# A float32 decoder layer on one core: first block product's operands from ScalarE and VectorE, block products in fixed order, plain down sums copied by VectorE

## The chip, the cores and the metric

The kernel runs on 1 core of one Trainium2 chip. The metric is the device time of one execution in microseconds (us). A core has a matrix engine (TensorE, PE in the profile), a vector engine (VectorE, DVE), an activation engine (ScalarE, ACT), a general engine (GpSimd, POOL) and a queue that issues most DMAs (SyncE, SP). Each engine runs its own list of instructions in a fixed order and waits at the head of that list; DMAs run beside them. TensorE's sums lie in banks of PSUM, everything else in SBUF.

## The reference

One decoder layer on x (1024 tokens by 1024 channels), all in float32:

```python
x = x + 0.5 * post1(swiglu_1(pre1(x)))
x = x + post_mix(hybrid_mixer(pre_mix(x)))
x = x + 0.5 * post2(swiglu_2(pre2(x)))

def swiglu(x, w_gate, w_up, w_down):          # 1024 -> 2816 -> 1024
    return (jax.nn.silu(x @ w_gate) * (x @ w_up)) @ w_down
```

`pre` and `post` are RMS norms with a gain. The mixer (a stick-breaking attention group beside an RWKV-7 group) is not touched by the change. The two feed-forward parts, FFN1 and FFN2, are the same code with other weights.

## The kernel before

A float32 product is made of three matmuls (`mm3`, L123): each operand is split into a rounded part "hi" and a rest "lo" = value - hi, and hi·hi, hi·lo, lo·hi add up in one PSUM bank. So each weight block and each activation block is first made into a pair of tiles, `wh` and `wl` for weights.

**Up part of an FFN** (`Ffn.up`, L463). The 2816 hidden channels are 22 blocks f of 128. Blocks f = 0 and 1 are "plain": two halves h of the tokens, each a gate product (bank X) and an up product (bank Z). `plain_evac` (L350) takes them out: Silu of the gate sum on ScalarE, times the up sum on VectorE, then `split` (hi on ScalarE, lo on VectorE) and two DMAs to DRAM (`hf_d`), through one tile `e{f}_{h}`. Blocks f = 2 to 21 go as 2x2 block matrices with seven products instead of eight. `product(f)` (L428) issues them as n = 1, 2, 5, 6, 4, 7, 3, 12 matmuls each; n = 1, 6 and 7 share the bank X, which ScalarE copies out between them (`f1p` L423 after n = 1, `f1u` L439 after n = 6, `f1v` L444 after n = 7). They need two sets of combined operands:
- for the inputs, once per FFN, `combine` (L240): nine sums of 128x2048 on VectorE and the four splits (hi on ScalarE, lo on VectorE) of n = 5, 6, 4 and 7, in a pool `xr` of five buffers R0 to R4;
- for the weights, for every f, `prep(f)` (L300): `load(f)` brings the raw gate and up block (`f1r`, 512 KB each), VectorE makes four sums of 128x512, hi goes to ScalarE for n = 2, 6, 7 and to GpSimd for the others, and all seven lo to GpSimd. `prep(f + 1)` runs beside `product(f)`; only f = 2 has no product to run beside.

After the sums, the space of `xr` goes to a pool `fu` (L463 on), which holds the tiles of the product stage, every fifth pair `wh`, `wl` among them.

**Down part** (`ffn_down`, L491). The hidden blocks f = 0 and 1 are a plain product (`f1df`): 16 groups of six matmuls through two banks A, each copied to the accumulator tile `f1acc` (L555). The others are seven products again, in steps (c, i): n = 1, 2, 5, 6, 3, 7, 4 (`f1dX`, `f1dZ`, `f1dY`), whose sums VectorE adds to `f1acc` (L511). Their weights are prepared by `prep(c, ...)` (L519): four loads `f1B`, sums on GpSimd (`f1T`, `f1B`), seven `f1dwh` on ScalarE (L536) and seven `f1dwl` on GpSimd (L537). The hidden operands `f1ho` are loaded by `hload` (L540).

The order in which instructions of the program's different parts stand on an engine is made by a scheduler, by when it reckons their inputs to be there; `tc.keep_in_program_order` pins an instruction to the order of the program. Names with f2 are the same tiles in FFN2. `x2x`, `x2X6p` and `x2X4h` belong to the norm and transposition of FFN2's input, which run while its plain products have begun.

## Time and profile before

| | us |
|---|---|
| median of 3 runs | 2215.29 |
| lowest, highest | 2211.8, 2218.39 |
| the profiled execution | 2211.98 |
| its span (first to last instruction) | 2210.3 |
| PE busy | 2094.5 (95%) |
| DVE, POOL, ACT busy | 1329.6, 1108.3, 817.2 |

All times in the rows are us from the start of the span of that one execution. A row of a timeline gives the start, the duration, the engine, the line, the operation with its output and input, and in brackets the idle time just before it with what ended it. Durations of neighbours overlap by a little, so what an instruction costs in a row of its kind is the distance of the starts. The granted TensorE clock (PEclk) is given as a share of full speed; it takes two levels, 1.2 and 2.4 GHz, so 0.50 is a stretch wholly at the lower one.

### The profile page before, as it was taken

Reading aid. Unit: us, or ns where it says so; the run is one execution under the profiler, and the core shown is the slowest. Engines: PE = TensorE matmul, PEld = TensorE weight load, DVE = VectorE, ACT = ScalarE, POOL = GpSimd, SP = SyncE. Lnnn points to the kernel's source line nnn. Section 1 sums busy time; section 2 is a strip of 40 time slices with the busy share of each in tenths; the row PEclk is TensorE's granted clock in tenths of the full one; section 3 lists DMA queues with packets and bytes.
Section 4 is the critical chain, followed back from the end, with each engine's and each line's share of the span. In section 5 each row is a group of like instructions: output and inputs, shape, how many; then the busy total and the mean of one; then the engine's idle time right before and its main releaser. Section 6 shows DMA issues by size and latency. Waiting matters only on the chain.

```text
span 2210.3 us, 30206 instructions
## 1 busy us (share of the span) xinstructions
PE 2094.5 (95%) x10976; PEld 1719.9 (78%) x10976; DVE 1329.6 (60%) x1873; ACT 817.2 (37%) x1412; POOL 1108.3 (50%) x897
## 2 busy tenths in 40 slices
PE   8899999989999999999999999898799999998998
PEld 6678888868887777687888887777678888877886
DVE  7667777624546545735537778546676767733556
ACT  5233333332105533324136667436323333332102
POOL 2866666658542345245211111221686666647734
PEclk9999999999999999999989999999899999999999
DMA  5244555568764355164665572443235555566765
GB/s 153 76 124 130 164 141 157 153 213 307 225 215 146 78 168 172 48 181 140 192 150 159 174 217 87 157 129 115 76 100 149 161 153 146 160 225 204 254 212 190
DMA packets 415476, 353.82 MB, mean 160 GB/s; under 512 B 35169, under 2 KB 337249, under 8 KB 415329
## 3 DMA queue, kind: packets, MB, share of 16 engines
q1 hardware_dynamic: 406800, 347.45, 52.3%
q10 hardware_dynamic: 8528, 4.46, 0.9%
q8 instruction: 87, 1.43, 0.3%
q14 instruction: 61, 0.49, 0.1%
HBM read 224.96 MB, written 126.88 MB: 159 GB/s over the span
## 4 chain that ended last, share of the span: by engine, by line
PE 76%; DVE 9%; issue 4%; ACT 4%; POOL 4%; DMA 2%; SPq 0%; DVEq 0%; ACTq 0%; POOLq 0%
PE pj L124 3%; PE pj L126 2%; PE pj L125 2%; PE f2X L124 2%; PE f1X L124 2%; PE f2X L125 2%; PE f2X L126 2%; PE f1X L126 2%; PE f1X L125 2%; PE a_512o L1430 2%; PE f2DY L125 2%; PE f1DY L125 2%; PE f2DY L124 2%; PE f1DY L126 2%; PE f2DY L126 2%
## 5 line engine op out<-in xcount | busy, mean ns | idle before, releaser
L112 POOL TENSOR_SCALAR wh<-wr 128x1024 fp32r<-128x1024 f32 x54 | 62.3, 1155 | 280.1 <-PE wod L126 66.1
L319 POOL TENSOR_TENSOR f1wl<-f1r,f1wh 128x512 fp32r<-128x512 f32 x100 | 141.2, 1424 | 15.9 <-ACT f1wh L316 12.7
L319 POOL TENSOR_TENSOR f2wl<-f2r,f2wh 128x512 fp32r<-128x512 f32 x100 | 139.3, 1406 | 13.0 <-ACT f2wh L316 9.7
L113 POOL TENSOR_TENSOR wl<-wr,wh 128x1024 fp32r<-128x1024 f32 x54 | 136.6, 2532 | 3.1 <-PE pj L126 0.2
L318 POOL TENSOR_SCALAR f2wh<-f2r 128x512 fp32r<-128x512 f32 x60 | 68.5, 1147 | 107.4 <-PE f2pX L125 38.8
L318 POOL TENSOR_SCALAR f1wh<-f1r 128x512 fp32r<-128x512 f32 x60 | 60.0, 1005 | 91.6 <-PE f1X L125 27.0
L511 DVE TENSOR_TENSOR f1acc<-f1dX,f1acc 128x512 f32<-128x512 f32 x64 | 44.3, 692 | 76.8 <-PE f1dX L126 76.8
L511 DVE TENSOR_TENSOR f2acc<-f2dX,f2acc 128x512 f32<-128x512 f32 x64 | 44.3, 692 | 76.5 <-PE f2dX L126 76.5
L1409 POOL TENSOR_SCALAR a_0B<-a_512B 128x1 f32<-128x1 f32 x32 | 15.4, 482 | 131.4 <-DVE a_512B L1410 98.8
L124 PE MATMUL pj<-x1X4h,wh 128*128 128x512 f32 x176 | 75.5, 429 | 0.5 <-DVE tw L925 0.5
L124 PE MATMUL pj<-x1X2h,wh 128*128 128x512 f32 x176 | 72.3, 411 | 0.6 <-DVE qkl L1120 0.5
L126 PE MATMUL pj<-x1X4h,wl 128*128 128x512 f32 x176 | 70.5, 401 | 0.0
L125 PE MATMUL pj<-x1X4l,wh 128*128 128x512 f32 x176 | 69.6, 396 | 0.0
L125 PE MATMUL pj<-x1X2l,wh 128*128 128x512 f32 x176 | 69.4, 395 | 0.0
L126 PE MATMUL pj<-x1X2h,wl 128*128 128x512 f32 x176 | 69.4, 394 | 0.0
L319 POOL TENSOR_TENSOR f1wl<-f1S,f1wh 128x512 fp32r<-128x512 f32 x40 | 63.1, 1587 | 1.6
L319 POOL TENSOR_TENSOR f2wl<-f2S,f2wh 128x512 fp32r<-128x512 f32 x40 | 62.4, 1569 | 1.7
L537 POOL TENSOR_TENSOR f2dwl<-f2B,f2dwh 128x1024 fp32r<-128x1024 f32 x20 | 47.6, 2406 | 20.0 <-ACT f2dwh L536 20.0
L537 POOL TENSOR_TENSOR f1dwl<-f1B,f1dwh 128x1024 fp32r<-128x1024 f32 x20 | 47.6, 2401 | 19.4 <-ACT f1dwh L536 19.4
L124 PE MATMUL wod<-wh,ymh 128*128 128x512 f32 x128 | 51.6, 403 | 1.1 <-DVE woacc L196 1.1
L126 PE MATMUL wod<-wh,yml 128*128 128x512 f32 x128 | 50.2, 395 | 0.6 <-DMA yml<-yl_d 0.6
L125 PE MATMUL wod<-wl,ymh 128*128 128x512 f32 x128 | 50.4, 394 | 0.0
(1448 smaller groups left out, 7098.7 us busy)
## 6 DMA issues: line engine op xcount, KB each, us to landing
f1ho<-f1hs_d SPq DMA_DIRECT2D x112, 256.0 KB, 4.6
f2ho<-f2hs_d SPq DMA_DIRECT2D x112, 256.0 KB, 4.0
f1hs_d<-f1h SPq DMA_DIRECT2D x56, 256.0 KB, 3.3
f1hs_d<-f1l SPq DMA_DIRECT2D x56, 256.0 KB, 3.0
f2hs_d<-f2h SPq DMA_DIRECT2D x56, 256.0 KB, 3.0
f2hs_d<-f2l SPq DMA_DIRECT2D x56, 256.0 KB, 2.9
wr<-in_w_in_dram SPq DMA_DIRECT2D x27, 512.0 KB, 3.9
f1r<-in_ffn_w_gate_dram SPq DMA_DIRECT2D x19, 512.0 KB, 4.9
```

Source lines behind the costliest of these rows:

```text
L112: nc.gpsimd.tensor_scalar(wh, raw, 1.0, 0.0, op0=ALU.mult, op1=ALU.add)
L113: nc.gpsimd.tensor_tensor(wl, raw, wh, op=ALU.subtract)
L124: nc.tensor.matmul(ps, lhsT=lh, rhs=rh, start=first, stop=False, **kw)
L125: nc.tensor.matmul(ps, lhsT=lh, rhs=rl, start=False, stop=False, **kw)
L126: nc.tensor.matmul(ps, lhsT=ll, rhs=rh, start=False, stop=last, **kw)
L318: nc.gpsimd.tensor_scalar(wh, src[n], 1.0, 0.0, op0=ALU.mult, op1=ALU.add)
L319: nc.gpsimd.tensor_tensor(wl, src[n], wh, op=ALU.subtract)
L511: nc.vector.tensor_tensor(quarter(tt, n), ps, quarter(tt, n), op=ALU.add)
L537: nc.gpsimd.tensor_tensor(wl, src[n], wh, op=ALU.subtract)
L1409: nc.gpsimd.tensor_scalar(B[:, w:w + 1], iv, 1.0, 0.0, op0=ALU.mult, op1=ALU.add)
L1430: nc.tensor.matmul(po[:, 0:P], lhsT=t.AT[:, k * P:(k + 1) * P], rhs=V[:, t.z0 // P + k, :], start=t.first and k == 0, stop=t.last and k == ...
```

## The change

Four things are changed, in both FFNs unless said otherwise.
- `prep_first(2)` takes the place of `prep(2)`: the weights of f = 2 get their sums and all lo parts on VectorE and all hi parts on ScalarE, none on GpSimd. It is a generator that is run in pieces between the pieces of `combine`. `load(3)` is issued before them instead of after `combine`.
- The plain tiles of the second token half (`e0_1`, `e1_1`) become one tile `ev`, a sixth one in the pool `xr` of five buffers; before, they lay in the pool `WP`. FFN2 (`late=True`) pins its first Silu.
- The first matmul of each k = 0 group of a block product is pinned, in `Ffn.mm` and in the down part's `mm`.
- The 16 copies of the plain down sums go from ScalarE (L555) to VectorE (L583).

```diff
-    def mm3(ps, lh, ll, rh, rl, first, last, **kw):
-        nc.tensor.matmul(ps, lhsT=lh, rhs=rh, start=first, stop=False, **kw)
+    def mm3(ps, lh, ll, rh, rl, first, last, pin=False, **kw):
+        i = nc.tensor.matmul(ps, lhsT=lh, rhs=rh, start=first, stop=False, **kw)
+        if pin:
+            tc.keep_in_program_order(i)
...
             lo(4, r2)
+            self.ev = rp.tile("xr", f"{self.nm}ev", [P, 2, 1024])
             yield
...
+        def prep_first(self, f):
+            G, U = self.raw.pop(f)
+            S = self.fr.tile("S", f"{self.nm}S{f}", [P, 1024])
+            S1, S2 = [self.half(S, i) for i in range(2)]
+            A11, A12, A21, A22 = G[:, 0:4], G[:, 4:8], U[:, 0:4], U[:, 4:8]
+            sums = {5: (S1, A21, A22, ALU.add), 6: (S2, S1, A11, ALU.subtract),
+                    7: (A21, A11, A21, ALU.subtract), 3: (A12, A12, S2, ALU.subtract)}
+            src = {1: A11, 2: A12, 5: S1, 6: S2, 4: A22, 7: A21, 3: A12}
+            for i, n in enumerate(PO):
+                if n in sums:
+                    d, x, y, op = sums[n]
+                    nc.vector.tensor_tensor(d, x, y, op=op)
+                wh, wl = self.slot()
+                nc.scalar.copy(wh, src[n])
+                nc.vector.tensor_tensor(wl, src[n], wh, op=ALU.subtract)
+                self.op[f, n] = wh, wl
+                if i % 2:
+                    yield
...
                 mm3(ps, wh[:, k, :], wl[:, k, :], xh[:, k, :], xl[:, k, :], first and k == 0, k == 3,
-                    skip_group_check=True)
+                    pin=k == 0, skip_group_check=True)
...
-            t = WP.tile("wr", f"{self.nm}e{f}_{h}", [P, 1024])
+            t = self.ev[:, f] if h else WP.tile("wr", f"{self.nm}e{f}_{h}", [P, 1024])
             s, hv = t[:, 0:HT], t[:, HT:]
-            nc.scalar.activation(s, pg, AF.Silu)
+            i = nc.scalar.activation(s, pg, AF.Silu)
+            if self.late and f == h == 0:
+                tc.keep_in_program_order(i)
...
-            comb = self.combine()
+            comb, first = self.combine(), self.prep_first(2)
             self.plain_mm(0, 1)
             self.plain_evac(0, 0)
             self.plain_evac(1, 0)
+            self.load(3)
+            next(first)
             next(comb)
+            next(first)
             self.plain_mm(1, 1)
             next(comb)
-            self.prep(2)
+            next(first)
+            next(first, None)
+            next(comb, None)
             self.plain_evac(0, 1)
             self.plain_evac(1, 1)
-            next(comb, None)
             self.fu = Pool(self.nm + "u", dict(wh=1, wl=1, tp=3, hv=6, sh=3, sl=2, s1=1))
-            self.load(3)
...
-                nc.scalar.copy(quarter(tt, n), ps)
+                nc.vector.tensor_copy(quarter(tt, n), ps)
...
-    F2 = Ffn("f2", a["ffn2_w_gate"][0], a["ffn2_w_up"][0], a["ffn2_w_down"][0])
+    F2 = Ffn("f2", a["ffn2_w_gate"][0], a["ffn2_w_up"][0], a["ffn2_w_down"][0], late=True)
```

**ScalarE at the start of FFN1's block products, before.** `f1e` is a plain tile, `f1r_2` and `f1r_3` the raw weights of f = 2 and 3, `f1p` the copy of bank X after n = 1; the second number of a name tells tiles apart.

```order
L360 CAST f1e_1_623<-f1e_1_623 128x512
L316 CAST f1wh_606<-f1S_596 128x512
L316 CAST f1wh_612<-f1r_2_449 128x512
L360 CAST f1e_1_630<-f1e_1_630 128x512
L423 COPY f1p_702<-f1X_676 128x512
L425 ACTIVATE f1p_702<-f1p_702 128x512
L435 COPY f1y_719<-f1DY_706 128x512
L316 CAST f1wh_653<-f1r_3_643 128x512
L439 COPY f1u_733<-f1X_676 128x512
```

**The same place after.**

```order
L339 CAST f1wh_616<-f1r_2_449 128x512
L339 CAST f1wh_624<-f1r_2_447 128x512
L385 CAST f1ev<-f1ev 128x512 x2
L319 CAST f1wh_658<-f1S_646 128x512
L319 CAST f1wh_652<-f1r_3_515 128x512
L448 COPY f1p_701<-f1X_675 128x512
L460 COPY f1y_718<-f1DY_705 128x512
L450 ACTIVATE f1p_701<-f1p_701 128x512
L319 CAST f1wh_664<-f1r_3_517 128x512
L464 COPY f1u_732<-f1X_675 128x512
```

Two splits of f = 3 (`f1wh_658`, `f1wh_652`) now stand ahead of the first copy out of bank X; `f1wh_652` lies in the pool `fu`, on the space that `ev` had, and waits until the four DMAs that write `ev` to DRAM have landed.

**SyncE's queue at the same place, before** (`f1e_1`, after it `f1ev`, is the second token half's plain result on its way to DRAM; `f1r_3`, `f1r_4` raw weights):

```order
L366 DMA f1hf_d<-f1e_0_508 128x4x128 x2
L366 DMA f1hf_d<-f1e_1_623 128x4x128 x2
L285 DMA f1r_4_672<-in_ffn_w_gate_dram 128x8x128
L366 DMA f1hf_d<-f1e_1_630 128x4x128
L285 DMA f1r_3_643<-in_ffn_w_gate_dram 128x8x128
L366 DMA f1hf_d<-f1e_1_630 128x4x128
L285 DMA f1r_4_674<-in_ffn_w_up_dram 128x8x128
L285 DMA f1r_3_645<-in_ffn_w_up_dram 128x8x128
```

**and after:**

```order
L288 DMA f1r_3_515<-in_ffn_w_gate_dram 128x8x128
L391 DMA f1hf_d<-f1e_0_508 128x4x128 x2
L288 DMA f1r_3_517<-in_ffn_w_up_dram 128x8x128
L288 DMA f1r_4_671<-in_ffn_w_gate_dram 128x8x128
L288 DMA f1r_4_673<-in_ffn_w_up_dram 128x8x128
L391 DMA f1hf_d<-f1ev 128x4x128 x4
```

The loads of f = 3 and f = 4 now stand ahead of the writes of the second token half.

**PE in the plain down part of FFN1, before:** the first matmuls of the seven products stood among the plain ones.

```order
L126 MATMUL f1df_5_3876<-wh_3721,f1hf 128x512
L124 MATMUL f1dZ_4003<-f1dwh_3770,f1ho_3927 128x512
L125 MATMUL f1dZ_4003<-f1dwl_3771,f1ho_3927 128x512
L126 MATMUL f1dZ_4003<-f1dwh_3770,f1ho_3927 128x512
L124 MATMUL f1dZ_4003<-f1dwh_3770,f1ho_3927 128x512
L125 MATMUL f1dZ_4003<-f1dwl_3771,f1ho_3927 128x512
L126 MATMUL f1dZ_4003<-f1dwh_3770,f1ho_3927 128x512
L124 MATMUL f1dY_4011<-f1dwh_3774,f1ho_3929 128x512
L124 MATMUL f1df_5_3884<-wh_3727,f1hf 128x512
```

**and after:**

```order
L128 MATMUL f1df_5_3875<-wh_3720,f1hf 128x512
L124 MATMUL f1df_5_3883<-wh_3726,f1hf 128x512
L127 MATMUL f1df_5_3883<-wl_3727,f1hf 128x512
L128 MATMUL f1df_5_3883<-wh_3726,f1hf 128x512
L124 MATMUL f1df_5_3883<-wh_3726,f1hf 128x512
L127 MATMUL f1df_5_3883<-wl_3727,f1hf 128x512
L128 MATMUL f1df_5_3883<-wh_3726,f1hf 128x512
```

The seven matmuls of `f1dZ` and `f1dY` moved behind the last `f1df`, after the first six of `f1dX`; FFN2 moves alike.

## Rows read from the trace of the kernel before

**Rows 1.** The page: busy time by engine, and the chain by engine.

```profile
PE 2094.5 (95%) x10976; PEld 1719.9 (78%) x10976; DVE 1329.6 (60%) x1873; ACT 817.2 (37%) x1412; POOL 1108.3 (50%) x897
...
PE 76%; DVE 9%; issue 4%; ACT 4%; POOL 4%; DMA 2%; SPq 0%; DVEq 0%; ACTq 0%; POOLq 0%
```

**Rows 2.** Waits of PE, whole span: who for whom, total us, times, longest.

```profile
PE f2X L124 <- POOL f2wh L318: 10.9, 2, 8.0
PE f2df L124 <- ACT f2acc L555: 6.1, 2, 4.5
```

**Rows 3.** Timeline of PE: FFN1's first block product to its third.

```profile
70.07 0.39 PE L124 MATMUL f1X<-X_0h,f1wh 128*128 128x512 f32 x1
...
91.36 0.80 PE L124 MATMUL f1X<-X_1h,f1wh 128*128 128x512 f32 x1 [4.92 <-ACT f1u L439]
...
125.37 0.39 PE L126 MATMUL f1DY<-X_1h,f1wl 128*128 128x512 f32 x1
125.60 0.39 PE L124 MATMUL f1X<-X_0h,f1wh 128*128 128x512 f32 x1
```

**Rows 4.** Timeline of SP's queue, FFN1's up part.

```profile
35.63 39.72 SPq L366 DMA_DIRECT2D f1hf_d<-f1e  x6
```

**Rows 5.** Timeline of POOL, FFN1's first weight split.

```profile
53.78 15.36 POOL L318 TENSOR_SCALAR f1wh<-f1r 128x512 fp32r<-128x512 f32 x1 [24.72 <-PE f1pX L125]
```

**Rows 6.** Timeline of DVE at the end of FFN1's input sums.

```profile
65.77 2.28 DVE L256 TENSOR_TENSOR f1L<-f1R,f1H 128x2048 fp32r<-128x2048 f32 x1
67.97 0.68 DVE L307 TENSOR_TENSOR f1S<-f1r 128x512 f32<-128x512 f32 x1
68.57 0.68 DVE L355 TENSOR_TENSOR f1e<-f1pZ,f1e 128x512 f32<-128x512 f32 x1
```

**Rows 7.** DMA issues from 70 to 100: KB each, median us to landing.

```profile
f1hf_d<-f1e SPq DMA_DIRECT2D x4, 256.0 KB, 3.2
```

**Rows 8.** The same from 84.5 to 86.2: the last of these writes.

```profile
f1hf_d<-f1e SPq DMA_DIRECT2D x1, 256.0 KB, 6.3
```

**Rows 9.** Timeline of PE: FFN2's transposes, first and third block product.

```profile
1539.31 0.69 PE L163 MATMUL x2X6p<-ident,x2x 128*128 128x128 f32 x2 [2.88 <-ACT x2x L666]
...
1574.58 0.80 PE L124 MATMUL f2X<-x2X2h,f2wh 128*128 128x512 f32 x1 [8.02 <-POOL f2wh L318]
...
1627.98 0.39 PE L124 MATMUL f2X<-x2X2h,f2wh 128*128 128x512 f32 x1
```

**Rows 10.** Timeline of ACT, in the norm of FFN2's input.

```profile
1531.74 1.28 ACT L354 ACT_TABLE_LOAD   x1
```

**Rows 11.** Timeline of DVE: the first of FFN2's input sums.

```profile
1546.76 2.28 DVE L258 TENSOR_TENSOR f2R<-x2X2h,x2X2l 128x2048 f32<-128x2048 f32 x1
```

**Rows 12.** Timeline of PE, FFN1's plain down part.

```profile
468.81 0.39 PE L124 MATMUL f1df<-wh,f1hf 128*128 128x512 f32 x1
...
489.18 0.50 PE L125 MATMUL f1dZ<-f1dwl,f1ho 128*128 128x512 f32 x1 [3.70 <-POOL f1dwl L537]
...
495.38 0.80 PE L124 MATMUL f1df<-wh,f1hf 128*128 128x512 f32 x1 [4.53 <-ACT f1acc L555]
...
504.90 0.39 PE L124 MATMUL f1dX<-f1dwh,f1ho 128*128 128x512 f32 x1
```

**Rows 13.** Windows: us, busy (count) PE, PEld, DVE, ACT, POOL, then PEclk, DMA share, GB/s.

```profile
495.00:500.00 5.00, 4.62 (x11) 3.66 (x12) 0.00 (x0) 3.32 (x6) 5.00 (x3) 0.50 0.04 12
```

**Rows 14.** Timeline of POOL, FFN1's plain down part.

```profile
493.73 2.34 POOL L537 TENSOR_TENSOR f1dwl<-f1T,f1dwh 128x1024 fp32r<-128x1024 f32 x1
496.03 7.07 POOL L537 TENSOR_TENSOR f1dwl<-f1B,f1dwh 128x1024 fp32r<-128x1024 f32 x3
```

**Rows 15.** Timeline of SP's queue at the same place.

```profile
501.19 8.11 SPq L544 DMA_DIRECT2D f1ho<-f1hs_d  x11
```

**Rows 16.** DMA issues from 501.0 to 501.5.

```profile
f1ho<-f1hs_d SPq DMA_DIRECT2D x1, 256.0 KB, 4.6
```

**Rows 17.** Timeline of DVE, FFN1's plain down part.

```profile
506.53 0.69 DVE L511 TENSOR_TENSOR f1acc<-f1dX,f1acc 128x512 f32<-128x512 f32 x1 [34.06 <-PE f1dX L126]
```

More of the change, by code (lines that the diff above doesn't have):

```diff
@@ L220, in layer_kernel, with __init__ @@
     class Ffn:
-        def __init__(self, nm, wg, wu, wd):
-            self.nm = nm
+        def __init__(self, nm, wg, wu, wd, late=False):
+            self.nm, self.late = nm, late
             self.wg = wg.rearrange("(k p) f -> p k f", p=P)
@@ L566, in mm @@
                 mm3(ps, ho[n][:, 0, k, :], ho[n][:, 1, k, :], wh[:, k, :], wl[:, k, :], first and k == 0, k == 1,
-                    skip_group_check=True)
+                    pin=k == 0, skip_group_check=True)
         for s_, (c, i) in enumerate(steps):
```

## The prediction

> **What bounds the kernel now.** I read the page first, then the waits of PE, then the timelines at the places that the change touches. PE is busy 95% of the span and is 76% of the chain that ended last [rows 1]: the kernel is bound by TensorE, and an edit pays only where it takes away a gap of PE, or a stretch at the lower clock behind a gap. Neighbouring matmuls stand 0.227 us apart at the upper clock [rows 3], so a block product of 12 takes 2.72 us and one f of seven 19.04 us. At the lower clock the distance is about 0.43 us (4.62 us busy for 11) [rows 13]. The change moves no matmul away; it can give back only gaps, and there are four places with them.
>
> **FFN1, start of the block products.** The first one starts at 70.07, right behind the plain products, and that of f = 4, from where PE runs without gaps, at 125.60 [rows 3]. Two f's need 38.1 us, so 108.2 would be the end without loss: 17.4 us are lost. The longest single gap, 4.92 us, waits for a copy of bank X on ScalarE [rows 3], which stood behind a split of f = 3 whose raw weights came late: their loads stood on SP behind writes, one of which held the queue's head for most of 39.72 us [rows 4]. After: `load(3)` is out of that queue's jam, and f = 2's operands come out of VectorE's own list. VectorE's cost per 128x2048 sum is 2.20 us and per 128x512 0.60 us (distances of starts) [rows 6]. From 54.76, where the sum ahead of the new instructions ends (five such steps before 65.77), stand 7 large and 16 small ones up to the last lo of `ev`: 7 x 2.20 + 16 x 0.60 = 25.0, so it ends at 79.8. Products n = 1, 2, 5 find their operands in time and run from 70.07 to 78.2. Then comes the **new wait**: n = 6 adds to bank X, which `f1p` must have left; `f1p` stands on ScalarE behind the split `f1wh_652`, and that waits until all four writes of `ev` have landed. On SP these stand behind the loads of f = 4. A write lands in 3.2 us as the median, in 6.3 us when it stands among loads [rows 7, 8]. The last write is issued at about 80.2, so it lands between 83.4 and 86.5; I take 85.2, because the loads stand right ahead of it. The split and the copy (0.6 us each, as the small DVE ones) follow: n = 6 starts at 86.4, a gap of 8.2 us. Behind a gap of 4.5 us the trace shows a stretch of 5 us at the lower clock [rows 12, 13], 12 matmuls at 0.43 instead of 0.227: 2.4 us. Products n = 6, 4, 7, 3 take 10.9 us, so f = 2 ends at 99.7, and f = 3, whose raw weights and operands are there by then, at 118.7. That is 125.6 - 118.7 = **7 us won** (3 to 11: the landing -1.8 or +1.3, and up to 4 us of gaps that f = 3 may keep).
>
> What GpSimd did for f = 2 is gone, 7 lo and 4 hi. Its first split took 15.36 us [rows 5], from 53.78 to 69.1, while VectorE ran sums with two SBUF inputs without a gap, and it ended when VectorE turned to a row with a PSUM input at 68.57 [rows 6]. So f = 3's first splits on GpSimd will not start before the `ev` rows that read PSUM, about 76.8. They are needed at 99.7, so this is covered.
>
> The Trainium skill, "Perfetto Trace Analysis", section "Optimizing Scalar/DVE Operations", speaks against this part: as GpSimd and VectorE share an SBUF read port, moving work between these two might not help. By that rule the starts' gain of 14.3 us would fall away, and the time would be 2204. The trace agrees that the two collide, by the 15.36 us above; what that can cost here, by rows, is the first rival.
>
> **FFN2, the same place.** Silu no longer stands between the norm's square roots; one table load is 1.28 us [rows 10], four of them go, two on the way to the last transposes, and with them two Silu of 0.60. So `x2x` comes over 3.2 us earlier, which covers the transposes' wait of 2.88 us [rows 9]: they start at 1536.4. The plain products behind them lose a stretch at the lower clock too. They ended at 1574.58 - 8.02 = 1566.56; without the 2.88, a further 0.35 and about 3 us of lower clock at 1560.2. VectorE's sums started at 1546.76 [rows 11], now about 4.5 earlier. 12 large, 20 small and 3 of 0.4 us are 39.6 us, the last lo of `ev` at 1581.9, landed at 1587, n = 6 at about 1588.4. Products 1, 2, 5 run 1560.2 to 1568.4, so the **gap is 20 us**, where the old one was 8.02 ahead of n = 1 with smaller ones after. n = 4, which stood ahead of n = 6 before, can't fill it since the order is pinned. From 1588.4: 10.9 + 2.4 + 19.0 gives f = 4 at 1620.7 against 1627.98 [rows 9]: **7.3 us won** (3 to 11).
>
> **The two plain down parts.** Before, PE ran from 468.81 to 504.90 with gaps of 3.70 (GpSimd's `f1dwl`) and 4.53 (the copies on ScalarE, behind `f1dwh` casts) and 5 us at the lower clock [rows 12, 13]. After, the copies are on VectorE, which was idle there for 34.06 us [rows 17]: 16 x 0.69 us beside a group of six matmuls of 1.36 us each, so they are hidden; without that cover 0.69 us a group. The 96 plain matmuls then end at 468.81 + 21.8 = 490.6. **What is late next** is GpSimd's chain, which doesn't change: it hands out the fourth `f1dwl` at 496.07 and the next three 2.36 us apart [rows 14], against 1.36 us that PE takes for a product. n = 1, 2, 5 run until 494.7, n = 6 waits 1.2, n = 3 and 7 wait 0.9 each, until 501.9. Next on PE is n = 1 of the second step; its `f1ho` load is issued at 501.19, behind a weight load on SP that waits for the same chain, and lands 4.6 us later [rows 15, 16]: a gap of 3.9. It runs from 505.8 to 507.1, and n = 4 of the first step to 508.5. Before, the same work ended at 504.90 + 41 x 0.227 = 514.2. 5.7 us won; gaps of 7 us in 11 may bring the lower clock again (-2.4). I take **4.5 for each FFN** (2.5 to 7); FFN2's gap behind the copies is as long, 4.5 [rows 2], and its timeline is the same to a few tenths.
>
> A copy on VectorE has one input, in PSUM; the adds of L511, which read PSUM too, ran beside GpSimd's chain at its 2.4 us a row [rows 14, 17], so I add nothing for GpSimd. The pins move no other matmul: elsewhere PE's list is what it was.
>
> **The sum.** 7 + 7.3 + 2 x 4.5 = 23.3 us off the profiled execution's 2211.98: 2188.7. Its median sister runs are 3.3 us slower; halfway between the two bases, I forecast 2190. The ends of the four terms, which will hardly all fall on one side, give 11 to 36 us.
>
> **The rivals.**
> 1. *VectorE and GpSimd collide, so that `ev` ends later.* Once VectorE reads PSUM, GpSimd gets in, and VectorE's small rows stretch. GpSimd can run only four rows of f = 3 before it needs `ev` gone: two of 0.6 and two of 1.25 us, so `ev` is at most 3.7 us later per FFN: 3.3 + 3.6 + 9 = 16 us, 2197. For it: the 15.36 us [rows 5]. Against: VectorE waits only if GpSimd is in first.
> 2. *The wait for `ev` doesn't bind* (f = 3's split finds room elsewhere). Then f = 2 and 3 run through: 17.4 in FFN1, and in FFN2 from 1568.4 the sums still hold n = 4 to about 1574 and the plain end stands at 1560.2, f = 4 at 1604: 24. With 9: 50 us, 2163. Against: the wait stands in the list.
> 3. *Slower: f = 3 starves behind the late n = 6.* GpSimd's splits of f = 3's n = 5 wait for the same landing, and all later ones queue behind. If they miss f = 3's turn, PE gets gaps like those of before in f = 3, some 6 us, and 3 at the lower clock per FFN; with a landing 6 us later the starts lose 7.5 each, the down parts keep 5 in all: 10 us slower, 2223. It decides from where the landing is some 12 us later than I put it in both FFNs. Against: 13 us lie between the landing and f = 3.
> 4. *The change doesn't do what it says:* in FFN1 the first product was on time already, so a ready first operand gives nothing there; if also the down parts only trade ScalarE's wait for GpSimd's, within 5 us of before.
>
> **How the numbers follow.** Forecast 0.72, rival 1 0.12, rival 2 0.06, rival 3 0.05, rival 4 0.05. The range 2178 to 2205 takes in rival 1 and most of the ends. A measurement can tell some 0.3% (6.6 us) from no change. Faster 0.88 (forecast nearly whole, rivals 1 and 2), same 0.07, slower 0.05.
>
> **What would show it.** Right: a gap of about 8 us ahead of n = 6 of f = 2 in FFN1 and about 20 in FFN2, put down to ScalarE's copy `p2` or the landing; no 8 us gap ahead of FFN2's n = 1; transposes x2X6p without a wait; plain down sums without a gap and 1 to 4 us gaps on GpSimd's `dwl` and the `ho` load behind them; f = 4 at about 119, and in FFN2 at about 1609 (1620.7, less the 11.5 won ahead of it). Wrong: gaps in f = 3, VectorE rows stretched before `ev`, GpSimd's down chain slower than 2.4 us a row, or gaps at places that the change doesn't touch.

## The result, and the profile after

The changed kernel takes 2189.66 us (median; 2188.91 to 2190.37), the kernel before 2213.9 beside it. The ratio is 0.9885, 95% interval 0.9865 to 0.9905: faster by 1.15%. The forecast was 2190.0.

The page of the changed kernel: its span, the busy times and the chain by engine.

```profile
span 2187.6 us, 30180 instructions
...
PE 2082.1 (95%) x10976; PEld 1714.0 (78%) x10976; DVE 1341.7 (61%) x1919; ACT 800.5 (37%) x1384; POOL 1057.3 (48%) x875
```

Against [rows 1] PE lost 12.4 us of busy time (stretches at the lower clock are busy time too), GpSimd 51 us of work, and the span is 22.7 us shorter. The waits of PE (engine, tile and line, who it waited for: total us, times, longest) answer to [rows 2]:

```profile
PE f2X L124 <- ACT f2p L448: 18.0, 1, 18.0
PE f1X L124 <- ACT f1p L448: 7.7, 1, 7.7
...
PE f2dX L124 <- DMA f2ho<-f2hs_d: 4.0, 1, 4.0
PE f1dX L124 <- DMA f1ho<-f1hs_d: 3.8, 1, 3.8
...
PE f1dX L127 <- POOL f1dwl L565: 1.9, 2, 1.3
```

The rows of before are gone, and these new ones stand in their place: one wait ahead of n = 6 in each FFN, and small ones in the down parts.

To see where the time went I cut the span at starts of PE's instructions that both kernels have. **S1**: start of the span to n = 1 of f = 4 in FFN1. **D1**: first `f1df` to the second step's `f1dZ`. **M**: from there to the first `f2pX` of FFN2's plain products (the rest of FFN1's down part, 188.8 to 189.0 us in every kernel here, then norms and mixer, where no code was changed). **S2**: from there to n = 1 of f = 4 in FFN2. **D2**: as D1, in FFN2. The three stretches left over (the products from f = 4 on, twice, and the tail) are 343.2, 343.2 and 194.1 us in every kernel here, to 0.6 us, but for two places told below (the runs f3_later and own_queue). All times are of one profiled execution each:

| kernel | S1 | D1 | M | S2 | D2 | median |
|---|---|---|---|---|---|---|
| before | 125.60 | 45.47 | 995.53 | 118.17 | 45.10 | 2213.9 |
| after | 119.03 | 42.63 | 992.86 | 110.32 | 42.29 | 2189.7 |
| copies_only | 127.78 | 42.81 | 1002.96 | 120.29 | 42.32 | 2208.5 |
| copies_back | 118.32 | 46.38 | 994.06 | 108.48 | 46.52 | 2198.0 |
| free_order | 111.33 | 41.67 | 992.11 | 103.48 | 42.60 | 2180.8 |
| no_ev_wait | 116.55 | 42.38 | 996.30 | 109.21 | 42.91 | 2188.8 |
| lo_on_gpsimd | 127.44 | 42.87 | 997.59 | 118.32 | 42.08 | 2211.2 |
| silu_free | 118.36 | 42.10 | 993.00 | 113.73 | 41.90 | 2196.6 |
| ho_ahead | 119.14 | 36.26 | 993.54 | 111.16 | 35.44 | 2176.9 |
| down_gaps | 118.86 | 42.57 | 1000.65 | 110.98 | 43.46 | 2190.4 |
| f3_later | 114.08 | 41.77 | 992.04 | 104.50 | 43.53 | 2183.6 |
| free_ho_ev | 108.97 | 36.39 | 999.20 | 100.74 | 36.43 | 2164.2 |
| own_queue | 117.78 | 42.07 | 993.52 | 109.35 | 41.82 | 2188.1 |
| load3_only | 120.84 | 44.60 | 1001.60 | 115.90 | 44.47 | 2207.3 |

Before to after: S1 6.57, D1 2.84, S2 7.85, D2 2.81 us shorter, 20.1 in all. The other 2.67 of the span's 22.7 lie in M, in the mixer and the norms, where nothing was changed: M ranges from 992.0 to 1003.0 over these executions. Two windows of the same 50 us of the mixer, before and copies_only, show how (PE busy with count, granted clock, DMA share, GB/s). Before:

```profile
1200.00:1250.00 50.00, 47.64 (x403) 0.97 0.63 183
```

and copies_only:

```profile
1200.00:1250.00 50.00, 46.67 (x361) 0.86 0.54 154
```

The same code (its start differs by under 3 us) ran 42 matmuls fewer at a granted clock of 0.86 instead of 0.97. So a median carries some us of this, and the stretches S and D of a trace show an edit more finely than the medians do. They scatter too. Where the up part is that of the changed kernel (after, copies_back, ho_ahead, down_gaps), S1 is 118.3 to 119.1 and S2 108.5 to 111.2; where the down part is (after, no_ev_wait, lo_on_gpsimd, silu_free, own_queue), D1 is 42.1 to 42.9 and D2 41.8 to 42.9. Before and copies_only, with one up part, differ by 2.2 in S1 and 2.1 in S2. So a difference of 1 us in one stretch, and of 2 in S2, shows nothing by itself.

**FFN1's start after**, PE (answers to [rows 3]):

```profile
70.53 0.39 PE L124 MATMUL f1X<-X_0h,f1wh 128*128 128x512 f32 x1
...
86.55 0.79 PE L124 MATMUL f1X<-f1H,f1wh 128*128 128x512 f32 x1 [7.69 <-ACT f1p L448]
...
91.79 0.40 PE L124 MATMUL f1DW<-f1H,f1wh 128*128 128x512 f32 x1
...
119.03 0.39 PE L124 MATMUL f1X<-X_0h,f1wh 128*128 128x512 f32 x1
```

One gap of 7.69 us ahead of n = 6, its 12 matmuls at the lower clock (86.55 to 91.79, 5.24 us instead of 2.72), then f = 2 and 3 without a gap. What held it, on VectorE, SP and ScalarE:

```profile
78.45 1.28 DVE L310 TENSOR_TENSOR f1S<-f1r 128x512 f32<-128x512 f32 x1
79.66 2.76 DVE L386 TENSOR_TENSOR f1ev<-f1ev 128x512 fp32r<-128x512 f32 x2
82.34 0.68 DVE L311 TENSOR_TENSOR f1S<-f1S,f1r 128x512 f32<-128x512 f32 x1
```

```profile
76.80 0.37 SPq L288 DMA_DIRECT2D f1r<-in_ffn_w_gate_dram  x1
77.36 0.43 SPq L288 DMA_DIRECT2D f1r<-in_ffn_w_up_dram  x1
78.67 4.13 SPq L391 DMA_DIRECT2D f1hf_d<-f1ev  x4
```

```profile
83.11 0.62 ACT L319 CAST f1wh<-f1S 128x512 fp32r<-128x512 f32 x1 [3.87 <-DVE f1S L311]
85.39 0.62 ACT L319 CAST f1wh<-f1r 128x512 fp32r<-128x512 f32 x1 [1.66 <-DMA f1hf_d<-f1ev]
85.91 0.58 ACT L448 COPY f1p<-f1X 128x512 f32<-128x512 f32 x1
```

ScalarE stands 1.66 us for the landing of `ev`, and before that 3.87 us for VectorE's sum, which stands behind the last lo of `ev` on VectorE's list.

**FFN1's down part after**, PE (answers to [rows 12]), and the granted clock of a window behind the last gap:

```profile
489.69 0.50 PE L127 MATMUL f1dX<-f1dwl,f1ho 128*128 128x512 f32 x1 [1.26 <-POOL f1dwl L565]
...
492.02 0.50 PE L127 MATMUL f1dY<-f1dwl,f1ho 128*128 128x512 f32 x1 [0.67 <-POOL f1dwl L565]
...
494.36 0.50 PE L127 MATMUL f1dX<-f1dwl,f1ho 128*128 128x512 f32 x1 [0.67 <-POOL f1dwl L565]
...
499.62 0.79 PE L124 MATMUL f1dX<-f1dwh,f1ho 128*128 128x512 f32 x1 [3.83 <-DMA f1ho<-f1hs_d]
...
504.83 0.40 PE L124 MATMUL f1dZ<-f1dwh,f1ho 128*128 128x512 f32 x1
```

```profile
500.00:505.00 5.00, 5.00 (x13) 0.53 1.03 388
```

The 96 plain matmuls run without a gap, the four gaps are those of the forecast, and the 12 matmuls behind the last one ran at the lower clock (0.53, against 0.50 in [rows 13]).

### The profile page after: what moved, and what is told of

The parts are those of the page before. It is cut to its first block, busy times and chain, and to the rows that moved or that the text cites. A ratio compares the mean times of both kernels' runs of the same rounds, so it can differ in the third digit from the quotient of the medians.

```text
span 2187.6 us, 30180 instructions
## 1 busy us (share of the span) xinstructions
PE 2082.1 (95%) x10976; PEld 1714.0 (78%) x10976; DVE 1341.7 (61%) x1919; ACT 800.5 (37%) x1384; POOL 1057.3 (48%) x875
## 4 chain that ended last, share of the span: by engine, by line
PE 77%; DVE 12%; ACT 4%; issue 3%; POOL 2%; DMA 2%; SPq 0%; DVEq 0%; ACTq 0%; POOLq 0%
PE pj L124 3%; PE f1X L124 3%; PE f2X L124 3%; PE f1X L128 2%; PE f1X L127 2%; PE f2X L127 2%; PE f2X L128 2%; PE pj L128 2%; PE pj L127 2%; PE f2DY L124 2%; PE f1DY L128 2%; PE f1DY L124 2%; PE f2DY L127 2%; PE f1DY L127 2%; PE f2DY L128 2%
## 5 line engine op out<-in xcount | busy, mean ns | idle before, releaser
L322 POOL TENSOR_TENSOR f1wl<-f1r,f1wh 128x512 fp32r<-128x512 f32 x95 | 130.5, 1386 | 13.0 <-ACT f1wh L319 9.7
L322 POOL TENSOR_TENSOR f2wl<-f2r,f2wh 128x512 fp32r<-128x512 f32 x95 | 130.5, 1386 | 13.0 <-ACT f2wh L319 9.7
L321 POOL TENSOR_SCALAR f2wh<-f2r 128x512 fp32r<-128x512 f32 x57 | 59.4, 1047 | 115.8 <-PE f2pZ L127 47.7
L321 POOL TENSOR_SCALAR f1wh<-f1r 128x512 fp32r<-128x512 f32 x57 | 49.0, 864 | 110.1 <-PE f1pZ L127 41.1
L322 POOL TENSOR_TENSOR f1wl<-f1S,f1wh 128x512 fp32r<-128x512 f32 x38 | 58.4, 1545 | 3.5 <-ACT f1wh L319 1.9
L124 PE MATMUL f2dX<-f2dwh,f2ho 128*128 128x512 f32 x128 | 50.9, 398 | 4.0 <-DMA f2ho<-f2hs_d 4.0
L124 PE MATMUL f1dX<-f1dwh,f1ho 128*128 128x512 f32 x128 | 51.1, 399 | 3.8 <-DMA f1ho<-f1hs_d 3.8
L127 PE MATMUL f1dX<-f1dwl,f1ho 128*128 128x512 f32 x128 | 51.0, 398 | 1.9 <-POOL f1dwl L565 1.9
```

The lines of the kernel that those rows point to most:

```text
L124: i = nc.tensor.matmul(ps, lhsT=lh, rhs=rh, start=first, stop=False, **kw)
L127: nc.tensor.matmul(ps, lhsT=lh, rhs=rl, start=False, stop=False, **kw)
L321: nc.gpsimd.tensor_scalar(wh, src[n], 1.0, 0.0, op0=ALU.mult, op1=ALU.add)
L322: nc.gpsimd.tensor_tensor(wl, src[n], wh, op=ALU.subtract)
```

## The experiments

**The copies alone (copies_only).** The kernel before with one line changed:

```diff
-                nc.scalar.copy(quarter(tt, n), ps)
+                nc.vector.tensor_copy(quarter(tt, n), ps)
```

> The kernel before with one edit alone: the sixteen copies of the plain down sums of each FFN are on VectorE. Theory (what the two traces show, 2.8 us for each FFN, since the gaps behind the plain sums stay on GpSimd's chain and the lower clock comes back): 5.7 us faster than the kernel before, 0.9974 of it; PE without a gap in the 96 plain matmuls, then gaps of about 1.2, 0.7, 0.7 and 3.8 us. Rival A (the sizes of the prediction, 4.5 us each): 9 us faster, 0.9959. Rival B (the copies stood beside other work and the gain of this place belongs to another edit): no change.

Measured: 2208.5 us, 0.9982 (0.9970 to 0.9995), 4.5 us faster. D1 45.47 to 42.81, D2 45.10 to 42.32, 5.4 in all: the theory, and rival A's 9 us is excluded by the interval. S1 and S2 of this execution, the slowest of 12 (2218.3), are 2.2 and 2.1 us longer, with no code changed there.

**The copies back (copies_back)** on ScalarE in the changed kernel, the same line the other way.

> The changed kernel with the copies of the plain down sums back on ScalarE, all else as changed. Theory: 5.7 us slower than the changed kernel, 18.6 us faster than the kernel before (0.9916), with the gap of about 4.5 us behind the copies back in both FFNs; the parts simply add. Rival A: 9 us slower than the changed kernel (15 us faster than before, 0.993). Rival B: as the changed kernel, 0.9885.

Measured: 2198.0 us, 0.9927 (0.9913 to 0.9941), so 8.3 slower than the changed kernel. D1 46.38 and D2 46.52 are 3.75 and 4.23 longer, 8.0. That is rival A's size, by another mechanism than its own. PE:

```profile
487.33 0.80 PE L124 MATMUL f1df<-wh,f1hf 128*128 128x512 f32 x1 [9.74 <-ACT f1acc L583]
```

In the kernel before, matmuls of the next products filled part of this wait (3.70 and 4.53 us of gaps in [rows 12]); with the products' order fixed PE stands 9.74 us in one piece. The parts don't simply add: the copies are worth 5.4 us in the old order and 8.0 in the fixed one.

**The free order (free_order).** The changed kernel without the pins of the products.

```diff
-                    pin=k == 0, skip_group_check=True)
+                    skip_group_check=True)
```

> The changed kernel without the fixed order of the block products. Its list on TensorE differs at two places, the start of each FFN: ahead of n = 6 of f = 2 now stand n = 4 of f = 2, n = 1 of f = 3 and the first matmuls of n = 2 of f = 3. Theory: n = 6 still waits for the landing of ev's writes, at 86.5 and about 1576, but two products of 2.7 us each are run in that wait, so each FFN wins 5.4 us, up to 7.8 with the stretch at the lower clock: 11 to 15 us faster than the changed kernel, 0.982 to 0.984 of the kernel before. Rival A (the fixed order is what keeps f = 3 from holding f = 2 up, and carries part of the gain): slower than the changed kernel by 5 us or more. Rival B (order is indifferent, the end of f = 3 is set by its operands): within 2 us of the changed kernel.

Measured: 2180.84 us, 0.9854 (0.9836 to 0.9871), 8.8 faster than the changed kernel. S1 is 7.7 and S2 6.84 shorter. The profiled execution is the lowest (2173.42; highest 2184.5), so its trace flatters the total. PE in FFN1:

```profile
78.16 0.39 PE L124 MATMUL f1DW<-f1H,f1wh 128*128 128x512 f32 x1
...
80.88 0.39 PE L124 MATMUL f1X<-X_0h,f1wh 128*128 128x512 f32 x1
...
86.56 0.50 PE L124 MATMUL f1Z<-X_0h,f1wh 128*128 128x512 f32 x1 [2.80 <-ACT f1wh L319]
...
87.13 0.41 PE L124 MATMUL f1X<-f1H,f1wh 128*128 128x512 f32 x1
```

n = 4 of f = 2 and n = 1 of f = 3 run in the wait, the gap left is 2.80 us, and no lower clock follows it. In FFN2 a gap of 9.29 us is left, ahead of n = 1 of f = 3, on GpSimd's split, with 12 matmuls at the lower clock behind it. By the trace the theory holds, by the medians the gain is under its 11 us: the fixed order, a part of the change, costs time at the starts. In the down parts the free list is the same as the fixed one.

**No wait for `ev`'s landing (no_ev_wait).** The tiles of the pool behind `ev` are laid so that ScalarE's split does not lie on it.

```diff
             self.fu = Pool(self.nm + "u", dict(wh=1, wl=1, tp=3, hv=6, sh=3, sl=2, s1=1))
+            for t in ("s1", "sl", "sh"):
+                self.fu.tile(t, f"{self.nm}x{t}", [P, HT])
```

> The changed kernel with the tiles of the pool that follows ev laid so that ScalarE's split f1wh of f = 3, n = 2, no longer lies on ev: it need not wait for ev's four writes to land. Theory: the wait ahead of n = 6 then ends with the next late thing, the copy behind the split of f = 3's n = 5, whose sum VectorE makes only after the last lo of ev; n = 6 comes 2 to 3 us earlier in each FFN, 4 to 6 us faster than the changed kernel (0.986 of the kernel before). Rival A (the landing is the whole wait, as the prediction had it): the gap of 7.7 us falls away, and of the 18.0 us all that lies behind the sums: some 15 us faster, 0.982. Rival B (something else holds ScalarE): no change.

Measured: 2188.82 us, 0.9883 (0.9866 to 0.9901): not to be told from the changed kernel by medians. In the trace the gaps shrink from 7.69 to 5.94 and from 18.04 to 16.17:

```profile
PE f2X L124 <- ACT f2p L448: 16.2, 1, 16.2
PE f1X L124 <- ACT f1p L448: 5.9, 1, 5.9
```

S1 is 2.5 and S2 1.1 shorter, 3.6 in all against the 4 to 6 expected; S2's part is within the scatter of that stretch. So the theory holds with a smaller size: the landing was the last 1.8 us of the wait. Next on ScalarE's list is the split that waits for VectorE's sum; the rows of FFN1's start above show that it is n = 6's sum (L311), not n = 5's. Rival A, the prediction's own reading, is out.

**The lo parts on GpSimd (lo_on_gpsimd).** The seven lo of f = 2's operands leave VectorE.

```diff
-                nc.vector.tensor_tensor(wl, src[n], wh, op=ALU.subtract)
+                nc.gpsimd.tensor_tensor(wl, src[n], wh, op=ALU.subtract)
```

> The changed kernel with the seven lo parts of f = 2's operands on GpSimd, the casts still on ScalarE, all else as changed; TensorE's list is the same. Theory (the start is decided by the wait of n = 6, and that by the end of VectorE's list, which loses 7 x 0.60 = 4.2 us): n = 1 waits for GpSimd, which gets in only when VectorE reads PSUM, until about 74 in FFN1 and about 1564 in FFN2, but n = 6 starts 3 to 4 us earlier than 86.5 and 1576.3; in all 2 to 8 us faster than the changed kernel, 0.985 to 0.988 of the kernel before. Rival A (the operands from VectorE carry the gain of the starts, as the prediction had it): their 17 us go again, 0.996. Rival B (the skill's sentence that moving work between these two might not help): within 2 us of the changed kernel.

Measured: 2211.22 us, 0.9994 (0.9982 to 1.0005), 21.6 slower than the changed kernel: rival A's size, and my theory fell. n = 1 started on time (70.34), but n = 6 stood until 94.96. In FFN2 n = 2 stood 7.87 us for GpSimd's second lo as well. SP and ScalarE show why:

```profile
83.00 0.37 SPq L288 DMA_DIRECT2D f1r<-in_ffn_w_gate_dram  x1
84.67 0.37 SPq L288 DMA_DIRECT2D f1r<-in_ffn_w_up_dram  x1
85.09 4.89 SPq L391 DMA_DIRECT2D f1hf_d<-f1ev  x4
```

```profile
93.80 0.62 ACT L319 CAST f1wh<-f1r 128x512 fp32r<-128x512 f32 x1 [9.56 <-DMA f1hf_d<-f1ev]
```

SP's list has f = 4's loads ahead of `ev`'s writes. They need the buffer of f = 2's raw weights, which GpSimd's last lo reads until 84.6. The last lo of `ev` was done at 81.8, but no write could go out before 85.09, and then all four were issued at once behind the two loads: 6.5 us as the median from issue to landing, against 3.2 in the changed kernel.

**The same, with f = 4's loads on GpSimd's own queue (own_queue).**

```diff
-                (nc.scalar if f == 2 else nc.sync).dma_start(t, w[:, :, c])
+                (nc.scalar if f == 2 else nc.gpsimd if f == 4 else nc.sync).dma_start(t, w[:, :, c])
```

> The run with f = 2's lo parts on GpSimd again (2211.2 us), with one edit: the two loads of f = 4 are issued on GpSimd's queue, not on SP ahead of ev's writes. In that run these loads stood at SP's head until GpSimd's last lo had read f = 2's weights (84.6 us), and the four writes behind them started 3.3 us after the last lo of ev was done. Theory (this queue is what the move to GpSimd costs): the writes go out as VectorE finishes, ev lands about 3 us behind the last lo at 81.8, and n = 6 starts at about 86 instead of 94.96 in FFN1 and 8 us earlier in FFN2; 14 to 17 us faster than that run, 0.992 of the kernel before. Rival A (VectorE and GpSimd slow each other's rows, and that is the cost): the landing is 3 us earlier at most, 5 us in all, 0.997. Rival B (GpSimd's own list holds it): no change, 0.9994.

Measured: 2188.07 us, 0.9899 (0.9878 to 0.9920), 23 us faster than the run before it. SP, ScalarE and PE:

```profile
78.71 3.53 SPq L391 DMA_DIRECT2D f1hf_d<-f1ev  x4
```

```profile
84.41 0.62 ACT L319 CAST f1wh<-f1r 128x512 fp32r<-128x512 f32 x1 [0.16 <-ACT f1wh L319]
```

```profile
85.56 0.79 PE L124 MATMUL f1X<-f1H,f1wh 128*128 128x512 f32 x1 [6.89 <-ACT f1p L448]
```

n = 6 at 85.56 (forecast 86), S1 9.7 and S2 9.0 shorter than with the loads on SP. (The tail is 195.0 us here.) The theory holds and rival A, the slowing of VectorE's and GpSimd's rows, does not: with the queue free, S1 and S2 are within 1.3 us of the changed kernel, where VectorE makes the lo parts. In FFN2 two waits stand for the one of 18.0 us, this one on GpSimd's second lo and then 6.12 ahead of n = 6:

```profile
1560.03 0.80 PE L128 MATMUL f2Z<-x2X2h,f2wl 128*128 128x512 f32 x1 [7.85 <-POOL f2wl L340]
```

The changed kernel itself with f = 4's loads on GpSimd's queue was not run. What the move between the two engines changes is who releases a buffer, and when.

**The load order alone (load3_only).** The kernel before with one line of the change:

```diff
             self.plain_evac(1, 0)
+            self.load(3)
...
-            self.load(3)
```

> The kernel before with one edit of the change alone: the loads of f = 3's raw weights are issued behind those of f = 2, ahead of the writes of the plain products, not behind them. Theory (the queue on SP is what the start of FFN1 lost, as the run with GpSimd's own queue says, and which engine makes f = 2's operands matters little): the gaps of 4.92, 3.49 and 2.23 us in f = 2 and 3 go, f = 4 starts at 117 to 121 instead of 125.6; in FFN2 the 8.0 us ahead of n = 1 stay and the later gaps of 2.9 and 3.9 us go; 9 to 15 us faster than the kernel before, 0.993 to 0.996. Rival A (the operands made by ScalarE and VectorE carry the gain of the starts): under 3 us, 0.9985 or more. Rival B (f = 3's splits, ready earlier, now stand ahead of f = 2's on GpSimd or ScalarE): slower than before.

Measured: 2207.26 us, 0.9976 (0.9963 to 0.9989), 5.7 faster than before. S1 is 4.76 shorter (f = 4 at 120.84, inside the forecast), S2 2.27, D1 and D2 0.9 and 0.6; M was 6.1 longer in this execution. So the load order by itself is worth 4.8 us in FFN1, more than rival A's 3; FFN2's 2.3 is hardly more than that stretch scatters, and the sum is less than the theory's (rival A's 0.9985 lies just inside the interval). In FFN2 the gap of 8.0 us stayed, and one of 6.77 ahead of n = 1 of f = 3 took the place of those of 2.9 and 3.9. In FFN1 a gap of 7.0 us stayed, on ScalarE, which in turn waited for VectorE:

```profile
88.09 1.73 DVE L313 TENSOR_TENSOR f1r<-f1r,f1S 128x512 f32<-128x512 f32 x1 [4.22 <-POOL f1wl L319]
```

VectorE's fourth sum of f = 3 overwrites raw weights that GpSimd's lo still reads, and f = 2's addition stands behind it. It is the order of these two that costs here, not how soon GpSimd comes to f = 3. In own_queue, with the seven lo of f = 2 on GpSimd, the same sum waits even longer for GpSimd, but the addition stands ahead of it:

```profile
85.54 0.69 DVE L449 TENSOR_TENSOR f1p<-f1Z,f1p 128x512 f32<-128x512 f32 x1 [0.36 <-ACT f1p L448]
93.04 0.69 DVE L316 TENSOR_TENSOR f1r<-f1r,f1S 128x512 f32<-128x512 f32 x1 [6.80 <-POOL f1wl L322]
```

**Silu not pinned (silu_free)** in FFN2.

```diff
-    F2 = Ffn("f2", ..., a["ffn2_w_down"][0], late=True)
+    F2 = Ffn("f2", ..., a["ffn2_w_down"][0])
```

> The changed kernel without the pinned first Silu of FFN2, so that Silu stands between the norm's square roots again. Theory (the prediction's step for FFN2): the transposes x2X6p wait 2.9 us again, VectorE's sums start 3 to 4.5 us later and with them the end of ev and n = 6 of f = 2: n = 6 at about 1580, 3 to 5 us slower than the changed kernel, 0.9905 of the kernel before. Rival (the 18 us wait of n = 6 hides it, or the transposes don't set VectorE's start): n = 6 stays where it is, within 1.5 us of the changed kernel.

Measured: 2196.57 us, 0.9919 (0.9905 to 0.9933). The transposes wait again:

```profile
1527.70 0.69 PE L165 MATMUL x2X6p<-ident,x2x 128*128 128x128 f32 x2 [2.88 <-ACT x2x L694]
```

From the first `f2pX` n = 6 starts after 82.26 us instead of 78.59, and S2 is 3.41 longer (6.9 by the medians): the theory, by the trace at the low end of its 3 to 5. The wait of 18 us hides nothing, since VectorE's list, which it waits for, moves along.

**The gaps of the down part, first try (down_gaps).** SP issues the next `ho` loads ahead of the next weights, and VectorE makes four of the first seven `dwl` behind the copies.

```diff
+            if s_ + 1 < len(steps):
+                hos[steps[s_ + 1]] = hload(*steps[s_ + 1])
             if i == 0 and c + 1 < NS:
                 prep(c + 1, blocks(c + 1))
-            if s_ + 1 < len(steps):
-                hos[steps[s_ + 1]] = hload(*steps[s_ + 1])
...
+        for wl, s, wh in lows:
+            tc.keep_in_program_order(nc.vector.tensor_tensor(wl, s, wh, op=ALU.subtract))
```

> The changed kernel with two edits in the down part: the loads of the next step's ho are issued ahead of the next weights on SP, and four of the seven dwl of the first block (n = 6, 3, 7, 4) are made by VectorE right behind the sixteen copies. Theory (the gaps behind the plain sums are GpSimd's 2.4 us a row and the late ho load, and the 12 matmuls at the lower clock follow from them): gaps of 1.2, 0.7, 0.7 and 3.8 us shrink to about 1.3 in all and the lower clock stays away; 5 to 7.5 us in each FFN, 10 to 15 us faster than the changed kernel, 0.982 to 0.984 of the kernel before. Rival A (only the gaps go, the lower clock comes again): 10 us at most, 0.984. Rival B (the next late thing stands right behind: ScalarE's casts or the weights of the second block): under 4 us, 0.987.

Measured: 2190.39 us, 0.9900 (0.9884 to 0.9915): rival B, nothing won. VectorE and PE:

```profile
484.66 1.31 DVE L588 TENSOR_TENSOR f1dwl<-f1T,f1dwh 128x1024 fp32r<-128x1024 f32 x1
485.90 8.67 DVE L588 TENSOR_TENSOR f1dwl<-f1B,f1dwh 128x1024 fp32r<-128x1024 f32 x3
494.49 0.68 DVE L539 TENSOR_TENSOR f1acc<-f1dX,f1acc 128x512 f32<-128x512 f32 x1
```

```profile
495.27 0.76 PE L124 MATMUL f1dX<-f1dwh,f1ho 128*128 128x512 f32 x1 [7.17 <-issue]
```

Three `dwl` took 8.67 us. One waited for ScalarE's cast, and GpSimd ran beside them, so that a row of 128x1024, 1.24 us by the distance of the first two starts, came to 2.9 as their mean. Bank X's addition stood behind them, and n = 6 needs that bank: one gap of 7.17 us for four of 6.4.

**The `ho` loads alone (ho_ahead),** the first half of that diff.

> The changed kernel with one edit in the down part: SP issues the loads of the next step's ho ahead of the next block's weights, which wait for GpSimd's chain. Theory (the 3.8 us gap is that load's place on SP, and the 12 matmuls at the lower clock follow from that gap alone): the three small gaps on GpSimd's dwl stay, the 3.8 us and the lower clock go, the second step's dZ starts 6.6 us earlier in each FFN; 11 to 13 us faster than the changed kernel, 0.983 of the kernel before. Rival A (the three small gaps of 2.6 us bring the lower clock by themselves): 4.2 us in each FFN, 8 us, 0.985. Rival B (the weights of the second block, now behind the ho loads, come late): later gaps in the first steps of the down part, gain under 4 us.

Measured: 2176.86 us, 0.9836 (0.9823 to 0.9850), 12.8 faster than the changed kernel. D1 36.26 and D2 35.44 are 6.4 and 6.9 shorter (forecast 6.6). PE and the window of before at the lower clock:

```profile
494.58 0.50 PE L127 MATMUL f1dX<-f1dwl,f1ho 128*128 128x512 f32 x1 [0.68 <-POOL f1dwl L565]
...
498.57 0.39 PE L124 MATMUL f1dZ<-f1dwh,f1ho 128*128 128x512 f32 x1
```

```profile
500.00:505.00 5.00, 5.00 (x24) 1.00 1.05 376
```

The three small gaps are still there (1.38, 0.67, 0.68), the 3.83 is gone, and with it the lower clock: a granted clock of 1.00 and 24 matmuls in the window where the changed kernel had 13. The theory holds in both its halves.

**f = 3 later (f3_later).** `prep(3)` behind `product(2)`, with the copies of f = 2's banks and the splits of f = 3 on ScalarE in the order of the code, and the layout of no_ev_wait.

```diff
-                if f + 1 < NF:
-                    self.prep(f + 1)
+                if 2 < f < NF - 1:
+                    if f == 3:
+                        self.prep(3)
+                    self.prep(f + 1)
```

> The changed kernel with the operands of f = 3 made behind the seven products of f = 2 in the list of ScalarE (the copies of f = 2's banks stand ahead of f = 3's splits), and with the tiles of the next pool laid so that none of f = 2's lies on ev. Theory (the wait of n = 6 is ScalarE's list: splits of f = 3 that wait for VectorE's sums and for ev's landing stand ahead of the copy of bank X): n = 6 follows n = 5 by 1.6 us in FFN1 instead of 7.7, without the lower clock, and by about 10.5 in FFN2 instead of 18.0, where ev's own splits still stand ahead; 13 to 18 us faster than the changed kernel, 0.981 to 0.983 of the kernel before. Rival A (f = 3's later operands starve TensorE behind f = 2): gaps in f = 3, gain under 5 us. Rival B (n = 6 waits for its own operands): n = 6 unchanged, no gain.

Measured: 2183.58 us, 0.9862 (0.9849 to 0.9876), 6 faster than the changed kernel, half of what the theory gave. n = 6 came as told (79.72 behind a gap of 0.96; in FFN2 a gap of 11.2), but n = 7 then waited 1.92 us for `f1u`, and the products from f = 4 on took 346.7 us instead of 343.2 in each FFN, with gaps such as 1.35 ahead of n = 7 of f = 4. S1 4.95 and S2 5.82 were won and 7 us of that given back: the mechanism is shown, the place for f = 3's operands was no better.

**Three together (free_ho_ev):** the free order, the layout of no_ev_wait and the `ho` loads ahead.

> Three edits together on the changed kernel: no fixed order of the products, the tiles laid so that ScalarE's split of f = 3 does not lie on ev, and the ho loads ahead of the weights. Theory (the waits are separate and add up): 9 us from the order, 1 to 3 us from the landing and 11 to 13 us from the ho loads, 21 to 25 us faster than the changed kernel, 0.974 to 0.978 of the kernel before. Rival A (the products that fill the wait already cover the landing, and the down part gives only its gaps): 15 to 18 us, 0.979 to 0.981. Rival B (they hide each other): under 12 us, above 0.983.

Measured: 2164.17 us, 0.9791 (0.9773 to 0.9809): 25.5 us faster than the changed kernel and 2.1% faster than the kernel before, the best version here. By the ratio it lies at rival A's edge, by the stretches the waits add: S1 is 10.06 shorter (7.70 and 2.48 alone), D1 and D2 6.2 and 5.9 (6.4 and 6.9 alone), S2 9.58; M was 6 longer than in the changed kernel. The longest wait left at these places is FFN2's gap of 9.2 us on GpSimd's split.

## Why the prediction was right, point by point

**The bound.** PE, and only its gaps and the lower clock behind them: with the same 10976 matmuls, the change in S1, S2, D1 and D2 is gaps and clock.

**FFN1's start: 7 forecast, 6.6 measured, with two errors that cancel.** n = 6 was put at 86.4 and came at 86.55, f = 4 at 118.7 and came at 119.03. But the last lo of `ev` ended at 82.3, not 79.8: 0.5 of that was there from the start, 2.1 is rival 1, since VectorE's three rows of 128x512 took 3.9 us instead of 1.8 while GpSimd ran beside them. And the landing took 3 us, not 5.4. The step that failed is "because the loads stand right ahead of it": they had been issued 1.3 us ahead, and did not slow the writes; lo_on_gpsimd shows the 6.5 us that I had feared, where they really go out together. no_ev_wait shows a third thing that I had not put in: without the landing VectorE's sum is next, 1.8 us earlier. One reading of the kernel before was incomplete: the six writes of [rows 4] left SP's head at 75.35, and from there to 82.97 f = 4's load stood at it, until GpSimd's lo had read f = 2's raw weights (its row ends at 82.95):

```profile
82.97 0.37 SPq L285 DMA_DIRECT2D f1r<-in_ffn_w_gate_dram  x1
```

f = 3's first load followed at 84.08. So the queue that lo_on_gpsimd shows had cost time in the kernel before already.

**FFN2's start: 7.3 forecast, 7.85 measured.** Counted from the first `f2pX`, n = 6 was forecast at 78.6 and came at 78.6, f = 4 at 110.9 and 110.3. The Silu's part is shown by silu_free (3.4 us); the load order's, 2.3 by load3_only, is near the scatter. Inside, the same two errors cancel (last lo of `ev` 2.2 later, landing 3.1 instead of 5.1), and the plain products ended 4.5 us earlier, not 6.4; the wait behind them hid that.

**The down parts: 4.5 each forecast, 2.8 measured. This term was mis-sized.** The gaps were right: 1.2, 0.9, 0.9 and 3.9 forecast, 1.26, 0.67, 0.67 and 3.83 measured. The step that failed is "may bring the lower clock again (-2.4)", of which I took half: it came in both FFNs, 5.2 us for 12 matmuls instead of 2.7 in FFN1 (499.62 to 504.83) and 4.8 in FFN2. ho_ahead shows that the three small gaps by themselves don't bring it. Some 0.4 us more in FFN1 are the `ho` load: issued at 494.75, 0.2 us later in the stretch than before, it landed after 4.9 us instead of 4.6. That GpSimd keeps its 2.4 us a row beside the copies is right (480.18 to 489.56 for four rows); [rows 14, 17], named for it, don't overlap in time.

**The sum.** The steps gave 23.3 us and the stretches that they speak of gave 20.1. The forecast of 2190 met the median because the mixer was faster too, by 2.7 us between the two profiled executions. The prediction knew nothing of it, so that the sum came out whole is luck. Whether this is scatter or follows from the change stays open. The stretch ranges over 11 us in these traces, with the same instructions; but of the 60 executions on record of the kernel before only 3 would be as fast as the slowest of the changed kernel's four if 20.1 us were taken off each, so scatter alone is not likely.

**"The pins move no other matmul."** True of PE's list, but for some plain matmuls and transposes of FFN2 that changed places, and the 20 us gap that n = 4 "can't fill" was foreseen; not worked out was what the pins cost, 14.5 us of S1 and S2 by the trace of free_order, 8.8 by the medians.

**What the starts' gain is made of.** From single edits, in us of S1 and S2: the load order 4.8 and 2.3 (load3_only), the lo parts off GpSimd 8.4 and 8.0 (lo_on_gpsimd against the changed kernel), the Silu 3.4 in FFN2 (silu_free), less 7.7 and 6.8 for the fixed order (free_order). That gives 5.5 of the 6.6 in FFN1 and 6.9 of the 7.9 in FFN2, as near as the stretches can tell. Parts need not add, as the copies show, and no run separates the hi parts on ScalarE or the tile `ev`.

**The rivals.** Rival 1 happened in its mechanism (2.1 of its 3.7 us) and not in its result. Rival 2 did not: the wait bound, though only 1.8 us of it was the landing. Rival 3 did not: f = 3 ran without a gap. In lo_on_gpsimd the landing came 8.4 us later, and even there FFN1's f = 3 had none; what cost 8 us for each FFN was the wait of n = 6 itself. Rival 4 did not, though its premise is true: FFN1's first product started at 70.53, no earlier than before.

**The rule that spoke against the change.** lo_on_gpsimd and own_queue differ by 23 us with the same instructions on the same compute engines, and own_queue is within 1.6 us of the changed kernel. The Trainium skill, "Perfetto Trace Analysis", section "Optimizing Scalar/DVE Operations", says that offloading between GpSimd and VectorE might not help. The runs agree with it for the lo parts taken by themselves; the 14.3 us that I let hang on it do not: part of them is the load order and the Silu, and what the move itself is worth, 8.4 and 8.0 us, is the place of f = 4's loads on SP's queue, which the move lets go sooner.

## What to carry to other kernels

When an operation moves to another engine, ask first which buffer its last read releases, which DMA waits at a queue's head for that buffer, and what stands behind that DMA: here that was 8 us in each FFN, while with that DMA on another queue the starts took the same time, to 1.3 us, with the operations on either engine. Cost a gap together with the stretch at the lower clock behind it, and look for the one gap that brings it: to issue one load earlier took away about 3.9 us of waiting and 2.1 to 2.5 us at the lower clock in each FFN. A fixed order of products removes the filling of waits too, so pin only where the free order is seen to do harm.
